# Folding the TensorE heads of the last row units, with one exponential over three heads

## The chip, the cores and the metric

The kernel runs on one core of one Trainium2 chip. The metric is the device time of one execution in microseconds, as the median of several runs; lower is better. The engines are named as in the profile: PE (TensorE's products), PEld (its weight loads), ACT (ScalarE), DVE (VectorE), POOL (GpSimd), SP (SyncE, which issues the loads).

## The reference

The input x has the shape 8 x 2048 x 2048, in float32. A row of 2048 columns is eight heads of 256 columns; each head has its own bias of 256 values. The result is, for every row and head, the logarithm of the sum of exponentials of x + bias, and each result is written twice:

```python
x_heads = x.reshape(B, S, H, Dh).transpose(0, 2, 1, 3)
x_heads = x_heads + bias[None, :, None, :]
x_tiled = np.repeat(x_heads, 2, axis=2)
mx = x_tiled.max(axis=-1, keepdims=True)
lse = mx.squeeze(-1) + np.log(np.exp(x_tiled - mx).sum(axis=-1))
```

The kernel takes no maximum: it sums exp(x + bias) directly, or exp(x) times exp(bias), and takes the logarithm at the end.

## The kernel before

**Tiles and loads.** The 16384 rows are 64 tiles of 256 rows (`T`), two rows on each of 128 partitions. Tiles lie in eight buffers (`NBUF`) and are loaded by SP, up to tile 41 in pairs of 4 MB, then singly, and from tile 57 on row by row. A row unit of 128 rows is 1 MB; the text calls the units of tile 62 "62a" and "62b", and so on. The two units of the last tile come in pieces of columns (`LAST_COLS`): 63a as columns 0-512, 1280-2048, 512-1280, and 63b in five pieces. A load waits for the last uses of the tile eight before it.

**Who adds the bias and who sums.** `STAGES` says from which tile on which mode holds. A mode's `pe` is the number of heads whose bias TensorE adds: `put_bias` (L284; L267 in the bulk) writes the bias rows into a PSUM bank as a product of three rows of ones, and `add_x` (L302; L326 in the bulk) adds x by a product with the identity matrix. ScalarE then takes the exponential out of PSUM; `sum_biased` (L357) does this for one head and gives its sum by an accumulator, which costs a second, short read-out instruction. Heads from `g0` on get their bias from GpSimd (L376). All other heads get no bias: ScalarE takes exp(x) in place (`exp_inplace`, L382), and VectorE multiplies by exp(bias) and sums in one instruction per head (`weigh`, L417). Of these, the last `fold` heads go to GpSimd instead: `fold` multiplies them by exp(bias) (L433), adds halves to halves until 32 columns are left (L441, three adds), and VectorE sums these 32 (`add_up`, L447).

- Up to tile 53 (`BULK`): three TensorE heads, four GpSimd heads, one scaled by VectorE, and one VectorE sum over seven heads (L401).
- Tiles 54 to 56 (`MIXED`): one TensorE head, four GpSimd heads.
- Tiles 57 to 61 (`PROMPT_F1`): two TensorE heads, five VectorE heads, one folded.
- 62a and 62b (`SINGLE_F1`): one TensorE head, six VectorE heads, one folded.
- 63a (`PROMPT_F2`): two TensorE heads, four VectorE heads, two folded. 63b (`TRIPLE`): three TensorE heads, five VectorE heads.

**What sets the order.** The whole order is written out by hand (`tc.manual_schedule()`): every engine runs its instructions in the order in which the loop over tiles and pieces emits them, and waits come from the data. Two lists put work off: `for_pe` holds `pe_part`, a unit's exponentials out of PSUM, which ScalarE runs behind the next unit's exponential; `for_pool` holds VectorE's sum of a fold and the next loads, which run at the start of the next unit. For each unit the loop emits TensorE's add, the next unit's bias (`put_bias`), six warming products (`keep_warm`, L317: three float32 products, two records each), `for_pool`, ScalarE's exponential, `for_pe`, and VectorE's products. PSUM has four banks in two pairs for these units; a bias may be written into a bank only after ScalarE has read what was there. `on_bank` takes away false dependences between two banks of a pair.

**The end.** Behind a batch, `finish` turns the sums by four transposes on TensorE (L461), and ScalarE takes the logarithm (L471). For the last batch `finish_last` does it with one transpose (L482), one logarithm (L488) and a store.

Of the kernel before, what the change touches and what calls it, by code (L numbers as in the profile page):

```python
# [12 lines left out]
ALU = mybir.AluOpType  # L13
# [19 lines left out]
BULK = dict(pe=3, acc=1, g0=4, late=True, fold=0)  # L33
MIXED = dict(pe=1, acc=1, g0=4, late=False, fold=0)
PROMPT_F1 = dict(pe=2, acc=2, g0=8, late=False, fold=1)
PROMPT_F2 = dict(pe=2, acc=2, g0=8, late=False, fold=2)
SINGLE_F1 = dict(pe=1, acc=1, g0=8, late=False, fold=1)
TRIPLE = dict(pe=3, acc=3, g0=8, late=False, fold=0)
FOLD = 32

# [1 line left out]
    (0, (BULK,)),  # L42
    (54, (MIXED,)),
    (57, (PROMPT_F1, PROMPT_F1)),
    (62, (SINGLE_F1, SINGLE_F1)),
    (63, (PROMPT_F2, TRIPLE)),
]

LAST_COLS = [
    [(0, 512), (1280, 2048), (512, 1280)],  # L50
    [(0, 512), (768, 1280), (1280, 1792), (512, 768), (1792, 2048)],
]

# [2 lines left out]
def kernel(  # L56
# [184 lines left out]
    n_ps = [0]  # L241


    bank_users = [[], []]

    def on_bank(i, ins):
        for j, u in bank_users[i // 2]:
            if j != i and u.ins.engine != ins.ins.engine:
                tc.declare_no_dep(ins.ins, u.ins, reason="another bank")
        bank_users[i // 2].append((i, ins))  # L250
        return ins

    def put_bias(m, k0, k1):

        if m["late"]:
            pair = pairs[n_ps[0] % 2]
            n_ps[0] += 1
            got = [one_ps, pair[:, 0:MM], pair[:, MM : 2 * MM]]  # L260

            parts = [(ones3, b3)]
            if n_ps[0] <= NEARLY:
                parts = [(ones3[0:1], bparts[:, i]) for i in range(3)]
            for h, p in enumerate(got):
                for i, (lhsT, b) in enumerate(parts):
                    nc.tensor.matmul(  # L267
                        p,
                        lhsT=lhsT,
                        rhs=each_row(b, h * Dh, Dh, K),  # L270
                        start=i == 0,
                        stop=False,
                    )
            return got + [pair]
        n = m["pe"] * Dh
        rows = min(k1 - k0, max(MM // n, 1))
        got = []
        for k in range(k0, k1, rows):
            for c in range(0, n, MM):
                w = min(n - c, MM)  # L280
                bank = n_ps[0] % len(ps)
                p = ps[bank][:, 0 : rows * w]
                n_ps[0] += 1
                mm = nc.tensor.matmul(  # L284
                    p,
                    lhsT=ones3,
                    rhs=each_row(b3, c, w, rows),
                    start=True,
                    stop=False,
                )  # L290
                on_bank(bank, mm)
                got.append((k, k + rows, c, w, bank, p))
        return got

    def add_x(m, t, k0, c0, c1, got):
# [3 lines left out]
        for ka, kb, c, w, bank, p in got:  # L299
# [10 lines left out]
            for i in range(0, (kb - ka) * w, Dh):  # L310
                k, cw = divmod(i, w)
                heads.append((ka + k, (c + cw) // Dh, bank, p[:, i : i + Dh], mm))
        return heads

    def keep_warm():
        for _ in range(NWARM):
# [112 lines left out]
    def fold(t, k, h0, h1, sums, after):  # L429


        v = xts[t % NBUF][:, k, h0 * Dh : h1 * Dh]
        done = nc.gpsimd.tensor_tensor(  # L433
            out=v, in0=v, in1=w_sb[:, h0 * Dh - W1 : h1 * Dh - W1], op=ALU.mult
        )
        on_x(t, done, [after])
        v = v.rearrange("p (h j) -> p h j", j=Dh)
        n = Dh
        while n > FOLD:
            n //= 2  # L440
            done = nc.gpsimd.tensor_tensor(  # L441
                out=v[:, :, 0:n], in0=v[:, :, 0:n], in1=v[:, :, n : 2 * n], op=ALU.add
            )
            on_x(t, done, [])

        def add_up():
            red = nc.vector.tensor_reduce(  # L447
# [55 lines left out]

    for_pool = []
    for_pe = []


    next_units = [
# [12 lines left out]
    for t in range(T):  # L521
# [4 lines left out]
        for k0, k1, c0, c1 in pieces(t):  # L526
# [5 lines left out]
            if m["late"]:  # L532
                pe_part = late_heads(m, t, bias_here, sums)
            else:
                heads = add_x(m, t, k0, c0, c1, bias_here)

                def pe_part(t=t, heads=heads, sums=sums):
                    for k, h, bank, p, mm in heads:
                        sum_biased(t, k, h, bank, p, mm, sums)

            if c0 == 0:
                if next_units and not m["late"]:
                    bias_there = put_bias(*next_units.pop(0))
                if t > T_PROMPT and m["g0"] == H:
                    keep_warm()
                if m["g0"] < H:
                    add = g_add(m, t, k0, k1)
                if t < T - 1 or k0 == 0:
                    flush(for_pool)
            if t == T_PROMPT and (k0, c0) == (0, 0):  # L550
                first_factors()
            h0 = max(c0 // Dh, m["pe"])
# [2 lines left out]
            if h0 < h1 and not m["late"]:  # L555
# [72 lines left out]
```

The softmax here doesn't subtract the row's maximum and nothing guards it: scores larger than these inputs give would overflow.

## Time and profile before

| | us |
|---|---|
| median of 4 runs (all: 325.65, 325.17, 325.19, 325.11) | 325.18 |
| the profiled execution | 325.65 |
| its span, first to last instruction | 323.5 |
| busy in the span: PE, DVE, ACT, POOL | 273.2, 283.9, 265.6, 287.7 |
| TensorE's mean granted clock | 0.903 |
| bytes read from HBM | 134.23 MB, mean 419 GB/s |

The span is what the views show; some 2 us of the time lie around it. The granted clock is the share of full speed that TensorE was given, and it was 1.00 or 0.50 in this trace. A line of the stretches gives the busy time of each engine between two times. A line of the chain gives start, length, and what the end was waiting for. A line in order of time gives start, length, engine, line of the kernel, operation, output and input, shapes, a count, and in brackets how long the engine was idle before and what ended it. A group gives the count, the busy time and the mean ns of one, the idle time before, and who ended it. TensorE's ends are modelled and its products are pipelined, so one starts before the one ahead has ended.

### The profile page before, as it was taken

To read this page: it belongs to the slowest core of one execution; us is meant where nothing else is said; L and a number is where in the kernel's file an instruction comes from. 1 tells how busy PE (TensorE), PEld (TensorE's weight loads), DVE (VectorE), ACT (ScalarE), POOL (GpSimd) and SP (SyncE) were. 2 spreads that over 40 slices of the span, in tenths; PEclk is the share of its full clock that TensorE was granted. 3 is DMA by queue.
4 is the path that set the end of the run, shared out by engine and by line. 5 is a ranking of instruction groups with operands and counts; after the bars stand their busy time and mean duration, and the time that the engine had idled before them with its cause. 6 is when DMAs were issued, how large, how long until landed. Compare 5 with 4: busy or idle time off the path is not lost.

```text
span 323.5 us, 2398 instructions
## 1 busy us (share of the span) xinstructions
PE 273.2 (84%) x691; PEld 104.0 (32%) x691; DVE 283.9 (88%) x306; ACT 265.6 (82%) x426; POOL 287.7 (89%) x120
## 2 busy tenths in 40 slices
PE   5999999889978779878679799698998897499984
PEld 2333333333323223323223233223333332135442
DVE  1037679999999998989998799998999999999995
ACT  1167679898978977879886989879898898989995
POOL 7939997999999899999999999999999999957874
PEclk9997789989997998979996979988999799559999
DMA  7999999999999999999999999999999999999994
GB/s 311 460 401 450 446 403 447 438 409 450 438 405 454 436 405 447 442 409 443 446 405 437 446 409 442 421 423 423 428 436 426 421 425 428 417 422 422 418 400 156
DMA packets 8830, 135.42 MB, mean 419 GB/s; under 512 B 1041, under 2 KB 1425, under 8 KB 2417
## 3 DMA queue, kind: packets, MB, share of 16 engines
q1 hardware_dynamic: 8720, 135.27, 98.4%
q8 instruction: 5, 0.08, 0.1%
q14 instruction: 7, 0.06, 0.0%
q10 hardware_dynamic: 98, 0.01, 0.0%
HBM read 134.23 MB, written 1.05 MB: 418 GB/s over the span
## 4 chain that ended last, share of the span: by engine, by line
DMA 34%; DVE 23%; PE 23%; ACT 18%; POOL 1%; issue 0%; SPq 0%; DVEq 0%
DMA xb<-in_x_dram 33%; DVE R L401 18%; ACT xb L382 11%; PE pair L326 8%; PE one_ps L326 4%; PE pair L267 3%; DVE xb L394 3%; ACT xb L357 2%; PE one_ps L267 2%; PE pair L302 2%; ACT xb L344 2%; DVE xb L417 2%; ACT res L471 2%; POOL xb L376 1%; ACT xb L337 1%; PE pair L219 1%
## 5 line engine op out<-in xcount | busy, mean ns | idle before, releaser
L376 POOL TENSOR_TENSOR xb<-xb,b_rep 128x2048 f32<-128x2048 f32 x57 | 257.6, 4542 | 20.6 <-DMA xb<-in_x_dram 20.6
L401 DVE TENSOR_REDUCE R<-xb 128x14 f32<-128x3584 f32 (+1 forms) x56 | 214.5, 3830 | 1.9
L382 ACT ACTIVATE xb<-xb 128x2560 f32<-128x2560 f32 (+5 forms) x77 | 157.3, 2052 | 10.0 <-POOL xb L376 10.0
L326 PE MATMUL pair<-xb,ident 128*128 128x512 f32 x216 | 116.5, 667 | 0.0
L326 PE MATMUL one_ps<-xb,ident 128*128 128x512 f32 x108 | 68.6, 721 | 9.1 <-DMA xb<-in_x_dram 8.9
L344 ACT ACTIVATE xb<-pair 128x1024 f32<-128x1024 f32 x54 | 55.9, 1036 | 24.2 <-PE pair L326 23.9
L326 PEld LDWEIGHTS pair<-xb,ident 128*128 128x128 f32 x216 | 47.3, 219 | 62.8 <-issue 62.8
L394 DVE TENSOR_TENSOR xb<-xb,w_ps 128x512 f32<-128x512 f32 x54 | 36.8, 681 | 27.1 <-ACT xb L382 26.8
L337 ACT ACTIVATE xb<-one_ps 128x256 f32<-128x256 f32 x108 | 40.3, 386 | 6.0 <-PE one_ps L326 6.0
L267 PEld LDWEIGHTS <-ones 3*128 3x128 bf16 (+1 forms) x192 | 16.7, 94 | 79.6 <-issue 70.3
L267 PE MATMUL one_ps<-b,ones 3*128 3x512 bf16 x49 | 18.5, 377 | 23.6 <-ACT xb L337 23.6
L267 PE MATMUL pair<-b,ones 3*128 3x512 bf16 x98 | 28.9, 374 | 0.0
L326 PEld LDWEIGHTS one_ps<-xb,ident 128*128 128x128 f32 x108 | 17.4, 202 | 31.5 <-issue 16.2
L302 PE MATMUL pair<-xb,ident 128*128 128x512 f32 (+1 forms) x36 | 21.6, 687 | 6.7 <-DMA xb<-in_x_dram 6.7
L337 ACT ACTIVATION_READ_ACCUMULATOR xb<-one_ps 128x1 f32 x108 | 22.9, 212 | 0.0
L417 DVE CUSTOM_DVE_ANT_0 xb<-xb,w_ps 128x256 f32<-128x256 f32 x61 | 22.4, 418 | 0.0
L441 POOL TENSOR_TENSOR xb<-xb 128x128 f32<-128x128 f32 (+3 forms) x39 | 13.8, 355 | 3.1
L433 POOL TENSOR_TENSOR xb<-xb,w_sb 128x256 f32<-128x256 f32 (+1 forms) x13 | 10.0, 772 | 5.7 <-ACT xb L382 5.1
L317 PE MATMUL tp<-ident 128*128 128x128 f32 x84 | 13.9, 304 | 0.0
L317 PEld LDWEIGHTS tp<-ident 128*128 128x128 f32 x84 | 11.3, 203 | 3.7 <-issue 3.3
L471 ACT ACTIVATE res<-tp 32x1024 f32<-32x1024 f32 x7 | 7.1, 1013 | 5.9 <-PE tp L461 5.9
L357 ACT ACTIVATE xb<-pair 128x256 f32<-128x256 f32 x33 | 11.9, 362 | 0.0
(42 smaller groups left out, 86.9 us busy)
## 6 DMA issues: line engine op xcount, KB each, us to landing
xb<-in_x_dram SPq DMA_DIRECT2D x20, 4096.0 KB, 21.8
xb<-in_x_dram SPq DMA_DIRECT2D x17, 2048.0 KB, 21.6
xb<-in_x_dram SPq DMA_DIRECT2D x12, 1024.0 KB, 22.0
xb<-in_x_dram SPq DMA_DIRECT2D x4, 256.0 KB, 13.2
out_dram<-res SPq DMA_DIRECT2D x1, 896.0 KB, 6.7
xb<-in_x_dram SPq DMA_DIRECT2D x2, 384.0 KB, 15.9
xb<-in_x_dram SPq DMA_DIRECT2D x2, 128.0 KB, 6.3
out_dram<-res_last SPq DMA_DIRECT2D x1, 128.0 KB, 1.7
```

What stands on the lines that cost most here:

```text
L267: nc.tensor.matmul(p, lhsT=lhsT, rhs=each_row(b, h * Dh, Dh, K), start=i == 0, stop=False,)
L302: mm = nc.tensor.matmul(p, lhsT=ident, rhs=xts[t % NBUF][:, ka:kb, c : c + w], start=False, stop=True,)
L317: nc.tensor.matmul(tp[:, 0], lhsT=ident, rhs=ident, start=True, stop=True)
L326: mm = nc.tensor.matmul(p, lhsT=ident, rhs=xts[t % NBUF][:, :, h * Dh : (h + 1) * Dh], start=False, stop=True,)
L337: act = nc.scalar.activation(out=xts[t % NBUF][:, k, 0:Dh], in_=got[0][:, k * Dh : (k + 1) * Dh], func=ACT.Exp, accum_out=sums[:, k, 0:1],)
L344: act = nc.scalar.activation(out=xts[t % NBUF][:, :, Dh : m["pe"] * Dh].rearrange("p k (h j) -> p h k j", j=Dh), in_=got[-1].rearrange("p ...
L357: act = nc.scalar.activation(out=xts[t % NBUF][:, k, h * Dh : (h + 1) * Dh], in_=p, func=ACT.Exp, accum_out=sums[:, k, h : h + 1],)
L376: add = nc.gpsimd.tensor_tensor(out=v, in0=v, in1=each_row(b_rep, c - G0, D - c, k1 - k0), op=ALU.add)
L382: return on_x(t, nc.scalar.activation(out=v, in_=v, func=ACT.Exp), [after])
L394: mul = nc.vector.tensor_tensor(out=f, in0=f, in1=each_row(w_ps, m["pe"] * Dh - W0, n, k1 - k0), op=ALU.mult,)
L401: red = nc.vector.tensor_reduce(out=sums[:, k0:k1, h0:H], in_=v.rearrange("p k (h j) -> p k h j", j=Dh), op=ALU.add, axis=mybir.AxisListTy ...
L417: ttr = nc.vector.tensor_tensor_reduce(out=v, in0=v, in1=w, scale=1.0, scalar=0.0, op0=ALU.mult, op1=ALU.add, accum_out=dst,)
```

## The change

In units 62a, 62b and 63a a new mode, `FOLDED`, takes the place of `SINGLE_F1` and `PROMPT_F2`. TensorE adds the bias to three heads (768 columns, a whole pair of banks). The new `exp_biased` takes their exponential in one ScalarE instruction over 768 columns, without accumulators, and GpSimd folds all three heads; since their bias is already in, the multiplication (L433 before) is left out. VectorE multiplies and sums the other five heads; no head without a TensorE bias is folded in these units.

The order changes too. In 62a and 62b the exponential out of PSUM runs directly behind the unit's own exponential, ahead of the next unit's. VectorE's sum of a fold is held back by one more unit (`held`). Units with three TensorE heads have no warming products any more, as `m["pe"] * Dh <= MM` is false for them. In all units from tile 54 on, the next unit's bias is emitted behind the warming products and behind `for_pe` instead of ahead of them. In 63a the first piece has 768 columns instead of 512 and the third 512 instead of 768. 63b is unchanged.

```diff
-PROMPT_F2 = dict(pe=2, acc=2, g0=8, late=False, fold=2)
-SINGLE_F1 = dict(pe=1, acc=1, g0=8, late=False, fold=1)
+FOLDED = dict(pe=3, acc=0, g0=8, late=False, fold=0)
...
-    (62, (SINGLE_F1, SINGLE_F1)),
-    (63, (PROMPT_F2, TRIPLE)),
+    (62, (FOLDED, FOLDED)),
+    (63, (FOLDED, TRIPLE)),
...
-    [(0, 512), (1280, 2048), (512, 1280)],
+    [(0, 768), (1280, 2048), (768, 1280)],
...
         n = m["pe"] * Dh
+        if n > MM:
+            n_ps[0] += n_ps[0] % 2
...
+    def exp_biased(t, k, n, heads):
+
+        _, _, bank, _, mm = heads[-1]
+        act = nc.scalar.activation(
+            out=xts[t % NBUF][:, k, 0 : n * Dh],
+            in_=pairs[bank // 2][:, 0 : n * Dh],
+            func=ACT.Exp,
+        )
+        on_bank(bank, on_x(t, act, [mm]), both=True)
+        return act
...
-        done = nc.gpsimd.tensor_tensor(
-            out=v, in0=v, in1=w_sb[:, h0 * Dh - W1 : h1 * Dh - W1], op=ALU.mult
-        )
-        on_x(t, done, [after])
+        done = after
+        if h0 * Dh >= W1:
+            mul = nc.gpsimd.tensor_tensor(
+                out=v, in0=v, in1=w_sb[:, h0 * Dh - W1 : h1 * Dh - W1], op=ALU.mult
+            )
+            done = on_x(t, mul, [done])
...
-                def pe_part(t=t, heads=heads, sums=sums):
+                def pe_part(t=t, m=m, k=k0, heads=heads, sums=sums):
+                    if m["acc"] == 0:
+                        done = exp_biased(t, k, m["pe"], heads)
+                        for_pool.append(fold(t, k, 0, m["pe"], sums, done))
+                        return
                     for k, h, bank, p, mm in heads:
                         sum_biased(t, k, h, bank, p, mm, sums)
...
-                if next_units and not m["late"]:
-                    bias_there = put_bias(*next_units.pop(0))
-                if t > T_PROMPT and m["g0"] == H:
+                if t > T_PROMPT and m["g0"] == H and m["pe"] * Dh <= MM:
                     keep_warm()
...
-                if t < T - 1 or k0 == 0:
+                if m["acc"] == 0 and for_pool and last_acc == 0:
+
+                    held = list(for_pool)
+                    for_pool.clear()
+                elif t < T - 1 or k0 == 0:
                     flush(for_pool)
+                last_acc = m["acc"]
...
-            if c0 == 0:
+            if m["acc"] == 0 and t < T - 1:
+                for_pe.append(pe_part)
+            if c0 == 0 or t == T - 1 and k0 == 0:
                 flush(for_pe)
+            if c0 == 0 and next_units and not m["late"]:
+                bias_there = put_bias(*next_units.pop(0))
...
+                if h0 < h1:
+                    flush(held)
...
-            elif heads:
+            elif heads and not (m["acc"] == 0 and t < T - 1):
                 for_pe.append(pe_part)
```

More of the change, by code (lines that the diff above doesn't have):

```diff
@@ L244, with on_bank @@
     bank_users = [[], []]
-    def on_bank(i, ins):
-        for j, u in bank_users[i // 2]:
-            if j != i and u.ins.engine != ins.ins.engine:
+    def on_bank(i, ins, both=False):
+        pair = i // 2
+        i = None if both else i
+        for j, u in bank_users[pair]:
+            if None not in (i, j) and j != i and u.ins.engine != ins.ins.engine:
                 tc.declare_no_dep(ins.ins, u.ins, reason="another bank")
-        bank_users[i // 2].append((i, ins))
+        bank_users[pair].append((i, ins))
         return ins
@@ L440, in fold @@
             n //= 2
-            done = nc.gpsimd.tensor_tensor(
+            add = nc.gpsimd.tensor_tensor(
                 out=v[:, :, 0:n], in0=v[:, :, 0:n], in1=v[:, :, n : 2 * n], op=ALU.add
             )
-            on_x(t, done, [])
+            done = on_x(t, add, [done])
         def add_up():
@@ L505 @@
     for_pe = []
+    held = []
+    last_acc = None
     next_units = [
```

## The prediction

> **What bounds the kernel now.** I read the load on each engine first, then the stretches of the end, then the chain that ended last, then the single rows of that chain. The loads use the DMA engines for nearly the whole span, but the last bytes are there before 318 us, and the change touches only the four row units behind that (62a, 62b, 63a, 63b). So the question is what the last 12 us wait for.
>
> ```profile
> q1 hardware_dynamic: 8720, 135.27, 98.4%
> ```
>
> Columns of the next view: stretch, its length, busy us (instructions) of PE, PEld, DVE, ACT, POOL, then granted clock, DMA share, GB/s.
>
> ```profile
> 300.00:305.00 5.00, 5.00 (x26) 2.96 (x26) 5.00 (x32) 5.00 (x13) 4.22 (x10) 1.00 1.02 424
> 310.00:315.00 5.00, 4.26 (x20) 2.31 (x20) 4.73 (x28) 5.00 (x14) 3.91 (x9) 1.00 1.03 393
> 315.00:320.00 5.00, 3.34 (x19) 2.13 (x18) 4.96 (x30) 4.78 (x17) 4.03 (x8) 1.00 0.73 256
> ```
>
> ScalarE (ACT) has no idle time and VectorE (DVE) almost none: both bound the end, so taking work from one alone gains little. The chain (start, length, what) shows the hand-over:
>
> ```profile
> 292.87 1.01 ACT res L471
> ...
> 310.58 1.59 ACT xb L382
> 312.17 0.71 ACT xb L357 x4
> 312.88 1.60 ACT xb L382
> 314.48 0.02 issue
> 314.50 0.42 DVE xb L417
> ...
> 319.83 0.14 DVE R_last L447
> ```
>
> From 293 to 314 ACT is the chain, from there VectorE's products, to 319.97. Single rows in order of time:
>
> ```profile
> 292.87 1.01 ACT L471 ACTIVATE res<-tp 32x1024 f32<-32x1024 f32 x1 [0.51 <-PE tp L461]
> 310.49 1.68 ACT L382 ACTIVATE xb<-xb 128x1792 f32<-128x1792 f32 x1
> 311.97 0.19 DVE L447 TENSOR_REDUCE R_last<-xb 128x1 f32<-128x32 f32 x1 [0.19 <-POOL xb L441]
> 312.34 0.70 PE L302 MATMUL pair<-xb,ident 128*128 128x256 f32 x2 [0.74 <-DMA xb<-in_x_dram]
> 314.06 1.02 PE L302 MATMUL pair<-xb,ident 128*128 128x512 f32 x2
> 315.02 0.49 PE L284 MATMUL pair<-b,ones 3*128 3x512 bf16 x2
> 317.85 1.65 POOL L441 TENSOR_TENSOR xb<-xb 128x256 f32<-128x256 f32 x3
> ```
>
> The first row is the one place where the saturated part of ACT stood still: 0.51 us for TensorE's transposes, which ran late behind half-clock work. The groups give what the new instructions cost:
>
> ```profile
> L344 ACT ACTIVATE xb<-pair 128x1024 f32<-128x1024 f32 x54 | 55.9, 1036 | 24.2 <-PE pair L326 23.9
> L441 POOL TENSOR_TENSOR xb<-xb 128x256 f32<-128x256 f32 x1 | 0.7, 725 | 0.1
> L441 POOL TENSOR_TENSOR xb<-xb 128x128 f32<-128x128 f32 x12 | 5.5, 457 | 0.9
> ```
>
> **The change, part by part.**
>
> *ACT.* Before, 62a to the end takes 16 exponentials, nine of them sums from PSUM (L357, one per 0.36 us). After, it takes 15, five of them sums. The columns are the same; four read-outs go, and 9.2 us of work becomes 8.9. Prices: 1280 columns lie between rows of 1536 (1466 ns) and 768 (827 ns), 0.83 ns a column: 1.25 us. The new 768 columns from PSUM: the 1024-column row is 1036 ns, less 256 x 0.83 = 0.82 us. The bounds are 0.78 (from the 357 ns sum row plus 512 columns) and 0.90; I take the row without a sum. Back to back, each starts 0.09 before the end of the one ahead.
>
> *TensorE.* A unit now needs two bias products and a 512- and a 256-column add. From the rows above: biases 0.23 + 0.20, add records 0.53 + 0.43 + 0.22 and 0.38 to the end of the last: 1.98 us, against 0.28 + 0.70. Each unit takes a whole pair of banks, so 62a's second bias waits for 61a's sum (310.58), 62b's first for 61b's sum (312.45). Behind a waiting bias stands the whole queue: its add, then the later units. 24 warming products (L317, 0.77 us a unit) go.
>
> *GpSimd.* Three multiplications go (0.73, 0.73, 1.28). Adds are over 384, 192 and 96 elements: (725 - 457) / 128 = 2.1 ns an element gives 0.99, 0.59 and 0.39, with two gaps of 0.08: 2.13 us a unit. Bounds: 1.65, the two-head row, with which VectorE's wait for it goes (325.2), and 2.5, half as much again, with which 62b's fold and all behind it come 0.74 later (326.3). I take the line through the two rows.
>
> *VectorE.* 20 products instead of 21, at 0.342 (rows 312.20 to 314.25 hold six), three sums over 96 elements instead of 32, 32, 64: about 0.17 against 0.10 of queue time, 0.25 for the last. Its work falls by 0.1 us.
>
> *The walk*, in the times of the profile, 62a's exponential starting at 310.49 as now:
> - ACT: 62a 310.49-311.74; 61b's two sums to 312.36; TensorE has 62a at 312.40, so the folded exponential runs 312.44-313.26. 62b 313.17-314.42. TensorE, held by 61b's sum, ends 62b at 314.50: folded 314.54-315.36 (wait 0.21). 63a's 768 columns 315.27-316.09; TensorE ends 63a at 316.41: folded 316.45-317.27 (wait 0.45). Then 512, 512, 512, 256 end at 317.79, 318.31, 318.83, 319.14; three sums end at 320.2.
> - GpSimd: 313.34-315.46, 315.47-317.60, 317.60-319.73.
> - VectorE: 61b's sum at 311.97, 62a's five products 312.07-313.78; waits for 62b's exponential, 314.45-316.16; sum of 62a's fold to 316.33; three products of 63a to 317.36; now **62b's fold (317.60) holds the queue**; sum to 317.82; two and five products to 320.21; last sum to 320.46.
>
> Against 319.96 that is +0.50: the folded exponentials ahead of 62b's own, and GpSimd, which starts 1.1 us later than now (313.34 against 312.24), put two waits of 0.67 and 0.27 into VectorE where it had none.
>
> *The stall at 292.87.* The warming products now come before the next bias. I count TensorE's full-height stream (products over 128 rows, not the three-row biases): 0.43 us for a 512-column record, 0.11 for a 128-column one, their spacing in the rows at full clock, and double at half. The clock's stretches are 3.41 us. In 284.86-288.28 this was an add (1.71 us) and the warming products up to the edge (0.65): 0.69 of the stretch, and the clock stayed at 0.50. The next held 0.76 and it rose. After, the add and all six (1.28) lie in the first: 0.87, so the clock should rise at 288.28, and the transposes be done well before ACT asks at 292.25. Then ACT's whole end moves 0.62 earlier (292.87 - 292.25); VectorE's queue is full until 311.70, its 62a then starts at 311.80, 62b's at 313.83, and the walk ends at 319.85.
>
> *Edits costed at nothing:* 63a's pieces of 384, 384, 256 KB instead of 256, 384, 384: three loads before and after on SP's queue, same bytes, 2.5 us a MB (TensorE's waits of 309.83 and 312.34), so they land by 313.3, 314.2 and 314.9, and the walk asks at 314.4 or later. The bias behind the warming in units 57 to 61: TensorE takes 2.04 a unit against ACT's 2.09 and fills banks units ahead; if that cover went, one bias and its switch, 0.31 a unit. VectorE's later sums: covered by products, except where the walk shows the fold late.
>
> *The sum.* The profiled execution took 325.65: its span of 323.5 and 2.15 around it. Its own stall removed and the walk's loss added: 325.65 - 0.11 = 325.54. The other three runs (325.11, 325.17, 325.19) are 0.47 faster. Without the stall the kernel before would itself end sooner: 62b's exponential would start when its load lands (312.30) and end at 314.0, VectorE at 319.48, that is 0.48 sooner. So I take those runs to have had no stall, and add 319.85 - 319.48 = 0.37 to the median of 325.18: **325.55 us**.
>
> *A rule against a row.* In 271.21-274.62 TensorE was busy 2.49 of 3.41 us, and the next stretch was granted 0.50: the clock fell without an idle stretch. The Trainium skill, "TensorE: Matmul & The Clock Gate", Part 1, says it falls back after at least one idle window of about 3.4 us. By the rule the end of the changed kernel, idle for 1.9 us at most, is safe and the sum stands at 325.55; by the row the third rival below stays possible.
>
> **The rivals.** 0.2% here is 0.65 us, about what a measurement can tell from no change. That the change does not do what it says I leave out: the changed kernel's instruction lists show the folded exponentials, the missing multiplications and the later sums where the code puts them.
> - *Stall gone only by the change* (B): the 0.47 between the runs is the profiler's cost and all runs before had the stall. For it: four runs can't tell. Then 325.18 - 0.11 = 325.07.
> - *Stall stays after the change* (C), because the clock's stretches lie otherwise: 320.46 against 319.48, 326.16.
> - *The clock falls in the tail* (D), the one that ends clearly slower. Between 61b's warming (ends near 308.95) and 62a's add (310.84, or 310.2 without the stall) TensorE has nothing tall to do. Stretches of the bulk whose full-height stream was up to 0.37 of 3.41 us were followed by 0.50, from 0.40 on by 1.00; a stretch from 308.95 to 312.36 would hold 1.28 us, 0.375. It decides from there. Against it: with the stretches where the profile has them (308.76) it is 0.43 or more. Price: 62b's and most of 63a's add at half rate, 63a's folded exponential 1.6 later, and the seven products behind it: 327.2.
> - *Better than walked* (E): TensorE's or GpSimd's waits don't arise. VectorE is still held by 62b's exponential, and 15 products and the sums behind it end at 320.10 - 0.62 = 319.5: no change. Faster by over 0.2% needs the stall to have been longer in the ordinary runs than in the profile: below 324.5.
>
> **How the numbers follow.** As forecast (325.55, own range 325.2 to 326.3 by GpSimd's bounds, which are the widest): 50 in 100, 6 of them above 325.83. B 18, C 14, D 12, E 6. Faster 0.06; slower 6 + 14 + 12 = 0.32; within 0.62. The range leaves out D and E: 324.9 to 326.4.
>
> **What would show it.** Right: folded exponentials near 0.82 us, the second and third waiting for TensorE; three GpSimd adds near 0.99, 0.59, 0.39; VectorE waiting once for ACT and once for GpSimd before its last seven products; no wait of L471's counterpart, and clock 1.00 from about 288. Wrong: VectorE without gaps to the end, ACT never waiting for TensorE, a half-clock stretch behind 309, or a last product that ends before 319.5.

## The result, and the profile after

The changed kernel takes **325.73 us** (median of 34 runs, 325.52 to 327.45), the kernel before, measured beside it, 325.37 us (55 runs, 325.07 to 326.71). The ratio is 1.0012, with a 95% interval of 1.0006 to 1.0018: slower by 0.2 to 0.6 us, and inside the 0.2% that the prediction took for no change. The forecast was 325.55, and the step from before to after +0.37; the medians differ by 0.36. The close agreement is partly luck: two errors in the working nearly cancelled, the waits that it named were not what cost the time, and the kernel before, which it took to run mostly without its stall, has a median of 325.37 and not 325.18.

The profiled execution took 325.71 us (span 323.7). First the stretches of the end, with the columns as before (stretch, length, busy us and instructions of PE, PEld, DVE, ACT, POOL, granted clock, DMA share, GB/s):

```profile
310.00:315.00 5.00, 4.74 (x15) 2.07 (x15) 4.81 (x24) 4.88 (x10) 3.23 (x8) 1.00 1.03 391
315.00:320.00 5.00, 2.92 (x10) 0.95 (x8) 5.00 (x29) 4.32 (x12) 4.13 (x7) 1.00 0.78 252
```

In the last 5 us ScalarE now has idle time (4.32 us busy against 4.78), VectorE none. The chain that ended last, start, length, what:

```profile
292.50 0.89 ACT res L488
...
308.00 1.38 ACT xb L397
...
311.47 0.19 DVE R_last L464
...
313.01 1.08 DVE xb L432
...
315.47 0.79 DVE xb L432
...
320.02 0.18 DVE R_last L464
```

From 311.47 to 320.19, where VectorE's last row ends, the chain is VectorE's own queue, without a wait. But two products in it take 1.08 and 0.79 us of the chain, where the others take 0.33. The same place as single rows, put together from the rows of ScalarE, GpSimd and VectorE in order of time:

```profile
292.39 1.00 ACT L488 ACTIVATE res<-tp 32x1024 f32<-32x1024 f32 x1
311.93 0.81 ACT L322 ACTIVATE xb<-pair 128x768 f32<-128x768 f32 x1
312.81 6.63 POOL L458 TENSOR_TENSOR xb<-xb 128x384 f32<-128x384 f32 x9 [1.38 <-ACT xb L322]
312.93 1.17 DVE L432 CUSTOM_DVE_ANT_0 xb<-xb,w_sb 128x256 f32<-128x256 f32 x1
314.02 0.81 ACT L322 ACTIVATE xb<-pair 128x768 f32<-128x768 f32 x1
315.40 0.86 DVE L432 CUSTOM_DVE_ANT_0 xb<-xb,w_sb 128x256 f32<-128x256 f32 x1
315.93 0.81 ACT L322 ACTIVATE xb<-pair 128x768 f32<-128x768 f32 x1 [0.37 <-PE pair L306]
316.19 0.24 DVE L464 TENSOR_REDUCE R_last<-xb 128x3 f32<-128x96 f32 x1
317.04 0.42 DVE L432 CUSTOM_DVE_ANT_0 xb<-xb,w_sb 128x256 f32<-128x256 f32 x1
317.39 0.24 DVE L464 TENSOR_REDUCE R_last<-xb 128x3 f32<-128x96 f32 x1
319.94 0.25 DVE L464 TENSOR_REDUCE R_last<-xb 128x3 f32<-128x96 f32 x1
```

What to see: the logarithm (L488) starts with no idle time in brackets, so the stall of 0.51 us is gone. The folded exponentials take 0.81 us, as forecast. The long products are those whose second input is `w_sb`: the factor of head 7, the only factor of these heads that lies in SBUF and not in PSUM. Both long ones run while GpSimd adds, and the sums of the folds (L464) have no wait at all. The groups of 312 to 320, kept apart by shape (count, busy us and mean ns, idle before), give GpSimd's adds and the two kinds of product:

```profile
L458 POOL TENSOR_TENSOR xb<-xb 128x384 f32<-128x384 f32 x3 | 3.2, 1064 | 1.4 <-ACT xb L322 1.4
L458 POOL TENSOR_TENSOR xb<-xb 128x192 f32<-128x192 f32 x3 | 1.9, 634 | 0.2
L458 POOL TENSOR_TENSOR xb<-xb 128x96 f32<-128x96 f32 x3 | 1.2, 385 | 0.2
...
L432 DVE CUSTOM_DVE_ANT_0 xb<-xb,w_ps 128x256 f32<-128x256 f32 x15 | 5.4, 410 | 0.0
L432 DVE CUSTOM_DVE_ANT_0 xb<-xb,w_sb 128x256 f32<-128x256 f32 x4 | 2.9, 716 | 0.0
```

The same groups in the kernel before, also 312 to 320:

```profile
L417 DVE CUSTOM_DVE_ANT_0 xb<-xb,w_ps 128x256 f32<-128x256 f32 x15 | 5.4, 417 | 0.0
L417 DVE CUSTOM_DVE_ANT_0 xb<-xb,one_ps 128x256 f32<-128x256 f32 x5 | 1.9, 418 | 0.1
...
L417 DVE CUSTOM_DVE_ANT_0 xb<-xb,w_sb 128x256 f32<-128x256 f32 x1 | 0.4, 422 | 0.0
```

`one_ps` and `w_ps` lie in PSUM, and the six products of 62a from 312.20 on are among these 20. There is one product by `w_sb`, at 319.40, as the very last: head 7 of the other units was folded there, and it was GpSimd that multiplied by `w_sb`. The change folds heads 0 to 2 instead, and so hands head 7 of 62a, 62b and 63a to VectorE.

### The profile page after: what moved, and what is told of

Its sections match the earlier page's. It is cut to its first block, busy times and chain, and to the rows that moved or that the text cites. A ratio compares the mean times of both kernels' runs of the same rounds, so it can differ in the third digit from the quotient of the medians.

```text
span 323.7 us, 2358 instructions
## 1 busy us (share of the span) xinstructions
PE 268.6 (83%) x676; PEld 102.1 (32%) x676; DVE 284.6 (88%) x304; ACT 265.3 (82%) x421; POOL 287.7 (89%) x117
## 4 chain that ended last, share of the span: by engine, by line
DMA 35%; DVE 20%; POOL 17%; PE 14%; ACT 13%; issue 0%; SPq 0%; DVEq 0%
DMA xb<-in_x_dram 34%; POOL xb L391 17%; DVE R L416 14%; ACT xb L397 9%; PE pair L341 5%; PE one_ps L341 3%; PE pair L269 3%; DVE xb L432 2%; DVE xb L409 2%; ACT xb L372 2%; PE one_ps L269 1%; PE pair L218 1%; DMA brow<-in_bias_dram 1%; ACT xb L352 1%; ACT xb L359 1%; ACT res L488 1%
## 5 line engine op out<-in xcount | busy, mean ns | idle before, releaser
L341 PE MATMUL pair<-xb,ident 128*128 128x512 f32 x216 | 114.5, 657 | 0.0
L341 PE MATMUL one_ps<-xb,ident 128*128 128x512 f32 x108 | 67.7, 712 | 10.7 <-DMA xb<-in_x_dram 10.7
L341 PEld LDWEIGHTS pair<-xb,ident 128*128 128x128 f32 x216 | 46.0, 213 | 61.7 <-issue 61.7
L306 PE MATMUL pair<-xb,ident 128*128 128x512 f32 (+1 forms) x42 | 23.7, 665 | 4.6 <-DMA xb<-in_x_dram 4.6
L458 POOL TENSOR_TENSOR xb<-xb 128x128 f32<-128x128 f32 (+5 forms) x39 | 16.4, 424 | 4.2 <-ACT xb L322 1.4
L306 PEld LDWEIGHTS pair<-xb,ident 128*128 128x128 f32 x42 | 7.1, 206 | 14.5 <-DMA xb<-in_x_dram 11.1
L450 POOL TENSOR_TENSOR xb<-xb,w_sb 128x256 f32<-128x256 f32 x10 | 7.3, 729 | 4.5 <-ACT xb L397 3.8
L332 PEld LDWEIGHTS tp<-ident 128*128 128x128 f32 x60 | 8.6, 198 | 7.4 <-issue 4.9
L372 ACT ACTIVATE xb<-pair 128x256 f32<-128x256 f32 x29 | 10.5, 367 | 0.0
L488 ACT ACTIVATE res<-tp 32x1024 f32<-32x1024 f32 x7 | 7.1, 1011 | 4.1 <-PE tp L478 4.1
```

What stands on the lines that cost most here:

```text
L306: mm = nc.tensor.matmul(p, lhsT=ident, rhs=xts[t % NBUF][:, ka:kb, c : c + w], start=False, stop=True,)
L341: mm = nc.tensor.matmul(p, lhsT=ident, rhs=xts[t % NBUF][:, :, h * Dh : (h + 1) * Dh], start=False, stop=True,)
L372: act = nc.scalar.activation(out=xts[t % NBUF][:, k, h * Dh : (h + 1) * Dh], in_=p, func=ACT.Exp, accum_out=sums[:, k, h : h + 1],)
L458: add = nc.gpsimd.tensor_tensor(out=v[:, :, 0:n], in0=v[:, :, 0:n], in1=v[:, :, n : 2 * n], op=ALU.add)
```

## The experiments

Theory P: the products by `w_sb` are held up by GpSimd's adds (they "stand"), and this is what the walk of the forecast lacked. Rivals: GpSimd's fold holds VectorE's sums (the forecast's own step), or the order of ScalarE costs the time. A second question is the stall before the logarithm, and whether the order of the bias took it away.

| kernel | us, median | before, beside it | ratio, 95% interval | us from the end of 62b's exponential to the end of VectorE's last row |
|---|---|---|---|---|
| changed | 325.73 | 325.37 | 1.0006 to 1.0018 | 6.30 |
| no folding adds | 325.47 | 325.40 | 0.9997 to 1.0022 | 6.04 |
| factor in PSUM from tile 59 | 325.78 | 325.40 | 1.0003 to 1.0025 | 6.70 |
| four moves | 325.30 | 325.36 | 0.9991 to 1.0014 | 5.73 |
| the factor's two moves alone | 325.61 | 325.41 | 1.0003 to 1.0024 | 6.04 |
| the order's two moves alone | 325.77 | 325.41 | 1.0006 to 1.0023 | 6.29 |
| folded exponentials late | 326.94 | 325.36 | 1.0031 to 1.0057 | 7.78 |
| changed, old order of the bias | 325.70 | 325.40 | 1.0003 to 1.0020 | 6.28 |
| before, new order of the bias | 325.15 | 325.40 | 0.9990 to 1.0020 | 5.50 |
| the same again | 325.29 | 325.41 | 0.9997 to 1.0030 | 5.50 |
| before, later logarithm | 325.65 | 325.36 | 1.0000 to 1.0017 | |
| before, both | 325.43 | 325.36 | 0.9995 to 1.0020 | |
| two folded units | 325.60 | 325.41 | 1.0003 to 1.0020 | 6.43 |

The last column is read from each profiled execution and leaves out what happened earlier in it. With no wait, the changed kernel's queue there is 15 products at 0.342, two sums at 0.17 and the last at 0.25: 5.72 us.

**GpSimd's nine adds left out.**

```diff
-        while n > FOLD:
+        while n > FOLD and h0:
```

> The changed kernel without GpSimd's nine additions in 62a, 62b and 63a; VectorE's three sums take the first 32 columns of each folded head as they are, so these heads' results leave out 224 of 256 columns. The eighth head's factor stays in SBUF. Theory P (a VectorE product with both inputs in SBUF stands until GpSimd's addition has ended): the eighth head's products take 0.42 us, and VectorE has only the waits for ScalarE left, ending near 319.9 instead of 320.19: 0.2 to 0.3 us faster than the changed kernel (1.0002 to 1.0006). Theory Q (another cause): the products stay long. If GpSimd alone were the bound of the end, the gain would be larger than 0.5 us, since its last addition ended at 319.45.

The four products by `w_sb` take 421 ns on average instead of 716, and VectorE now stands only for ScalarE:

```profile
312.87 0.42 DVE L432 CUSTOM_DVE_ANT_0 xb<-xb,w_sb 128x256 f32<-128x256 f32 x1
313.86 0.42 DVE L432 CUSTOM_DVE_ANT_0 xb<-xb,w_ps 128x256 f32<-128x256 f32 x1 [0.56 <-ACT xb L397]
315.23 0.42 DVE L432 CUSTOM_DVE_ANT_0 xb<-xb,w_sb 128x256 f32<-128x256 f32 x1
317.22 0.42 DVE L432 CUSTOM_DVE_ANT_0 xb<-xb,w_ps 128x256 f32<-128x256 f32 x1 [0.20 <-ACT xb L397]
```

So it is GpSimd's adds that make them long. The 0.74 us of 62a's product bought little, since VectorE then waits 0.56 for 62b's exponential; the 0.44 of 62b's counted, less 0.20 that VectorE then waits for 63a's. Seven of the 11 runs lie below the lowest of the changed kernel's 34 (325.52).

**The factor of head 7 in PSUM from tile 59 on.**

```diff
-            w = w_sb[:, c - W1 : c - W1 + Dh]
+            w = one_ps[:, 0:Dh]
...
+        if t == 59:
+            nc.vector.tensor_copy(one_ps[:, 0:Dh], w_sb[:, W2 - W1 :])
```

> The changed kernel, with the factor of the eighth head (columns 1792 to 2048) copied once, by VectorE in tile 59, into a half of a PSUM bank whose factor is no longer needed, and read there by VectorE's products; before it lay in SBUF. Theory P (a VectorE product with both inputs in SBUF stands until GpSimd's running addition has ended): the eighth head's products take 0.42 us instead of 1.17 and 0.86, VectorE is through 62b's products by 315.7 instead of 316.2, then waits for GpSimd's fold of 62b near 317.2 as the prediction had it, and ends near 320.05 instead of 320.19: the median falls by 0.05 to 0.2 us against the changed kernel (1.0006 to 1.0010 against the kernel before). Theory Q (these products are long for another cause, such as the unit's exponential or a bank of PSUM): they stay long and the time stays 1.0012.

The products took 414 to 417 ns while GpSimd added, and GpSimd's own first adds 998 to 1010 ns, the second ones 592 instead of 634. The time did not fall, though Theory P had expected it to: the copy took 0.42 us of a VectorE that is nearly full from tile 57 on, and in this execution its whole queue was late (its last long sum, over the GpSimd heads ahead of tile 57, ran at 292.34, in the changed kernel at 290.51). The cause of the length was shown, its worth was not; in the next two runs the copy lies in a gap, and the third leaves the factor where it was.

**Four moves in the tail.** 62a's head 7 first, before GpSimd adds; the copy behind 62a's products, where VectorE waits anyway; 63a's folded exponential behind its last own exponential; VectorE's sum of 62b's fold behind all of 63a's products.

```diff
+    first_w7 = []
...
+        elif not first_w7:
+            first_w7.append(t)
+            w = w_sb[:, c - W1 : c - W1 + Dh]
         else:
-            w = w_sb[:, c - W1 : c - W1 + Dh]
+            w = one_ps[:, 0:Dh]
...
-            if c0 == 0 or t == T - 1 and k0 == 0:
+            if c0 == 0 or t == T - 1 and k0 == 0 and c0 == 3 * Dh:
                 flush(for_pe)
...
-                    for h in range(h0, hf):
+                    hs = list(range(h0, hf))
+                    if (t, k) == (T - 2, 0):
+                        hs = hs[-1:] + hs[:-1]
+                    for h in hs:
...
-                if h0 < h1:
+                if h0 < h1 and (t < T - 1 or c0 == 3 * Dh):
                     flush(held)
+                if (t, k0) == (T - 2, 0):
+                    nc.vector.tensor_copy(one_ps[:, 0:Dh], w_sb[:, W2 - W1 :])
```

> The changed kernel with four places in its tail moved, each after a wait or a long product that its trace shows: 62a's head 7 is multiplied first, before GpSimd adds; the factor of head 7 is copied to PSUM in VectorE's gap behind 62a's products, so that 62b's and 63a's head 7 read one operand from PSUM; 63a's folded exponential stands behind its last own exponential; VectorE's sum of 62b's fold stands behind all of 63a's products. Theory P (VectorE's products with both inputs in SBUF stand while GpSimd adds, 0.74 and 0.44 us too long): the three products take 0.42 us each, VectorE ends about 319.6 instead of 320.19, and the time is 325.2 to 325.3 us, 0.9993 to 1.0000 of the kernel before. Rival (what is saved on VectorE goes into its waits for the exponentials and for GpSimd): VectorE ends at 320.0 to 320.2 again, 325.6 to 325.75 us, 1.0006 to 1.0014.

```profile
312.18 0.81 ACT L322 ACTIVATE xb<-pair 128x768 f32<-128x768 f32 x1 [0.24 <-PE pair L306]
314.18 0.42 DVE L437 CUSTOM_DVE_ANT_0 xb<-xb,w_ps 128x256 f32<-128x256 f32 x1 [0.49 <-ACT xb L397]
319.62 0.25 DVE L469 TENSOR_REDUCE R_last<-xb 128x3 f32<-128x96 f32 x1
```

From 62b's exponential to the end VectorE needs 5.73 us, which is the sum without any wait. It ends at 319.87 and not at 319.6 because TensorE gave 62a's bank 0.24 late in this execution. The chain shows from when:

```profile
293.43 0.94 PE tp L332 x6
294.36 0.32 PE pair L288
294.68 1.73 PE pair L306 x2
...
310.65 1.50 PE pair L306 x4
```

TensorE had waited 1.35 us for ScalarE's logarithm (the warming products write the tile that it reads), its granted clock was 0.50 from 294.93 to 298.35, an add took 1.73 us of the chain instead of 1.06, and up to 312 TensorE did not catch up. Such a half-clock stretch behind the logarithm stands in three of the 14 traces here (this one, and the runs below with the folded exponentials late and with two folded units), all with the new order of the bias. The loss is gone (325.30 beside 325.36, and seven of the 11 runs below the changed kernel's lowest), but no gain is shown either.

**The factor's two moves alone.** Of the diff above only `weigh` with `first_w7`, the list `hs` and the copy; the order as changed:

```diff
+                    hs = list(range(h0, hf))
+                    if (t, k) == (T - 2, 0):
+                        hs = hs[-1:] + hs[:-1]
...
+                if (t, k0) == (T - 2, 0):
+                    nc.vector.tensor_copy(one_ps[:, 0:Dh], w_sb[:, W2 - W1 :])
```

> The changed kernel with only the first two of the four moves of the run before it (62a's head 7 first; the factor of head 7 copied to PSUM in VectorE's gap), its order otherwise as changed. Theory P (the products that stand for GpSimd cost the most of the loss, and with them gone the wait for GpSimd's fold of 62b comes up, as the prediction had it): 62b's products start at 313.9 and end at 315.7, three of 63a at 316.8, VectorE then waits 0.2 to 0.4 for GpSimd's fold (317.0 to 317.2), and ends at 319.9 instead of 320.19: about 325.45 us, 1.0001 to 1.0007 of before. Rival (the factor's place alone is worth the whole gain of the four moves): 325.3 us, and VectorE does not wait for GpSimd.

The products by either place of the factor, and then the rows in which VectorE waits:

```profile
L437 DVE CUSTOM_DVE_ANT_0 xb<-xb,one_ps 128x256 f32<-128x256 f32 x3 | 1.3, 418 | 0.0
...
L437 DVE CUSTOM_DVE_ANT_0 xb<-xb,w_sb 128x256 f32<-128x256 f32 x1 | 0.4, 415 | 0.0
```

```profile
314.01 0.42 DVE L437 CUSTOM_DVE_ANT_0 xb<-xb,w_ps 128x256 f32<-128x256 f32 x1 [0.22 <-ACT xb L397]
317.17 0.25 DVE L469 TENSOR_REDUCE R_last<-xb 128x3 f32<-128x96 f32 x1 [0.18 <-POOL xb L463]
319.76 0.25 DVE L469 TENSOR_REDUCE R_last<-xb 128x3 f32<-128x96 f32 x1
```

This is the tail that the forecast had walked: with the long products gone, VectorE has 0.64 us for ScalarE, 0.42 of it filled by the copy (0.67 was forecast), and waits 0.18 for GpSimd's fold of 62b (0.27 was forecast). So the wait of Theory P came (0.2 to 0.4 was expected), but not its time: 325.61 instead of 325.45. Beside the changed kernel's 325.73 a gain is not clear of the noise; only one of the 11 runs lies below 325.52. From the start of 62a's exponential (310.07) to the end (320.02) are 9.95 us; the walk had 309.87 and 319.85, 9.98.

**The order's two moves alone.** The other half, with the factor in SBUF:

```diff
-            if c0 == 0 or t == T - 1 and k0 == 0:
+            if c0 == 0 or t == T - 1 and k0 == 0 and c0 == 3 * Dh:
                 flush(for_pe)
...
-                if h0 < h1:
+                if h0 < h1 and (t < T - 1 or c0 == 3 * Dh):
                     flush(held)
```

> The changed kernel with only the last two of the four moves (63a's folded exponential behind its last own exponential; VectorE's sum of 62b's fold behind all of 63a's products), head 7's factor in SBUF as changed. Theory P: the products of head 7 stand for GpSimd as in the changed kernel (about 1.16 and 0.86 us), VectorE ends at 320.1 to 320.2, 325.65 to 325.75 us, 1.0009 to 1.0013 of before. Rival (the order of ScalarE and of the sums costs the loss, not the factor's place): VectorE ends at 319.7 to 319.9, 325.3 to 325.4 us.

```profile
L432 DVE CUSTOM_DVE_ANT_0 xb<-xb,w_sb 128x256 f32<-128x256 f32 x4 | 2.9, 714 | 0.0
```

ScalarE's last sum ends 0.6 us earlier than in the changed kernel (318.99 against 319.60, 0.12 of it by an earlier start), and VectorE's tail is as long as there (6.29). The order alone shows no gain; it pays once the products are short, when it takes the wait for GpSimd away: 6.04 to 5.73, one trace each.

**The folded exponentials late:** those of 62a and 62b behind the next unit's own exponential, as the kernel before orders them.

```diff
-            if m["acc"] == 0 and t < T - 1:
-                for_pe.append(pe_part)
...
-            elif heads and not (m["acc"] == 0 and t < T - 1):
+            elif heads:
```

> The changed kernel with one thing put back: the folded exponentials of 62a and 62b stand behind the next unit's own exponential on ScalarE, as the kernel before has them, and GpSimd folds as in the changed kernel. Theory W (ScalarE's order is paid for by GpSimd's room): 62b's exponential starts with its landing, about 312.3, and ends about 313.55 instead of 313.895, so VectorE waits less for it; but GpSimd's first add starts about 314.35 instead of 312.81, its nine adds (three times 1.00 + 0.66 + 0.39, and one of 1.19) end about 320.95 instead of 319.45, and VectorE's last sum of the folds ends about 321.3 instead of 320.19: about 326.8 us, 1.0040 to 1.0048 of the kernel before. Rival (ScalarE's order alone costs the loss): GpSimd's later start is hidden, VectorE ends 0.3 to 0.4 earlier than in the changed kernel: about 325.3 us, 0.9995 to 1.0002.

```profile
312.52 1.27 ACT xb L397
313.79 0.71 ACT xb L322
...
314.56 1.01 POOL xb L458
...
321.32 0.27 DVE R_last L464
```

62b's exponential starts with its landing, and GpSimd 1.75 us later than in the changed kernel (314.56 against 312.81). From there GpSimd is the chain to the end, and VectorE's last sum waits 0.77 us for it. So the early place of the folded exponentials is paid for (62b's exponential starts at 312.63 in the changed kernel and at 312.52 here, where its load landed at 312.49), but it is the cheaper of the two.

**The order of the bias.** First the changed kernel with the bias ahead of the warming products again, as far as the banks allow it; then the kernel before with only the new order.

```diff
+                early = bool(next_units) and not m["late"] and t < 61
+                if early:
+                    bias_there = put_bias(*next_units.pop(0))
...
-            if c0 == 0 and next_units and not m["late"]:
+            if c0 == 0 and next_units and not m["late"] and not early:
                 bias_there = put_bias(*next_units.pop(0))
```

> The changed kernel, with the old order of the next unit's bias up to tile 60 (ahead of the warming products and of the work put off); the folded units keep the new one, since their banks need it. Theory 1 (the new order takes the stall away): the stall of about 0.5 us before the seventh batch's logarithm is back in the trace, the clock rises a stretch of 3.41 us later, and the median is 0.1 to 0.5 us above the changed kernel's, so about 326.0 against 325.73 (1.0015 to 1.0028 against the kernel before). Theory 2 (the order does nothing in ordinary runs): 1.0012 as the changed kernel.

```diff
-                if next_units and not m["late"]:
-                    bias_there = put_bias(*next_units.pop(0))
...
+            if c0 == 0 and next_units and not m["late"]:
+                bias_there = put_bias(*next_units.pop(0))
```

> The kernel before, with only the new order of the next unit's bias: behind the warming products and behind the work put off, in all units from tile 54 on. Modes, folds and pieces stay as before. Theory 1 (the stall behind the half-clock transposes was part of the ordinary runs, more in some than in others): the logarithm of the seventh batch no longer waits for TensorE, the clock is at 1.00 from about 288 us on, and the median falls by 0.1 to 0.5 us against the kernel before (0.9985 to 0.9997), to its fastest runs near 325.1; the runs lie closer together. Theory 2 (the ordinary runs had no stall, the profiled one was slow by the profiler): no change, 1.0000 within 0.0003. Theory 3 (the bias behind the warming costs TensorE 0.31 us a unit): ScalarE waits for TensorE in units 57 to 61 and the time rises by 0.3 us or more.

> The kernel before with the new order of the bias alone, once more. If that order takes the stall before the logarithm away in most runs: again most runs at 325.04 to 325.2 us, median 0.1 to 0.25 below that of before. If the first answer was chance: a median within 0.05 of before.

In the kernel before with the new order, the logarithm and the last sum:

```profile
292.39 1.00 ACT L471 ACTIVATE res<-tp 32x1024 f32<-32x1024 f32 x1
319.28 0.22 DVE L447 TENSOR_REDUCE R_last<-xb 128x2 f32<-128x64 f32 x1
```

No stall, and VectorE ends at 319.50, where the forecast put the kernel before without its stall (319.48); the repeat ends at 319.49. The clock did what the prediction had worked out. The next two lines are the same stretch, first of the kernel before (TensorE's busy time, then clock, DMA share and GB/s), then with the new order (all engines):

```profile
288.28:291.69 3.41, 3.41 (x9) 0.50 1.02 423
288.30:291.70 3.40, 3.40 (x17) 1.91 (x16) 3.40 (x14) 3.40 (x4) 1.15 (x2) 1.00 1.01 422
```

In these two traces the stretches of the clock lie within 0.04 us of each other, and the full clock came at 288.24 instead of 291.69 (288.28 was forecast). The half clock in this part lasted five stretches of 3.41 us in the kernel before and in its run with the later logarithm below, and three or four in all 11 traces with the new order. The changed kernel with the old order is the exception: four stretches, which lay 1 us later, no stall in its trace, and the same 325.70. Of the runs of the kernel before, 21 of 97 in these comparisons lie at 325.20 or below; with the new order 13 of 23 do, and the others at 325.39 to 327.72. So the order seems to make the undisturbed case more frequent. That it makes the kernel faster is not established: both intervals reach over 1. Nor do the runs lie closer together, which the first theory had also expected: three of the 23 take 327.58 us or more.

**The logarithm three tiles later,** in the kernel before, alone and with the new order of the bias:

```diff
-        fb, at = divmod(t - 2, NBLK)
+        fb, at = divmod(t - (5 if t > T_PROMPT else 2), NBLK)
```

> The kernel before with the finish of batch 7 (transposes, logarithm, store) three tiles later, and nothing else: the transposes then come when the exponentials they follow have long been fed, whatever TensorE's clock does at 288. Theory S (the stall before the logarithm is in most ordinary runs of before, and is what its median stands above its fastest runs by): median about 325.1 us with the runs close together, 0.9990 to 0.9996 of before. Rival (the spread of the runs has another cause): 325.35 to 325.45 us, 0.9998 to 1.0003, spread as in before.

> The kernel before with the later finish of batch 7 and with the changed kernel's order of the bias (the warming products and the adds of the pairs ahead of it). Theory S: with the stall gone by the later finish the order of the bias is worth nothing more: the same 325.1 us as with the later finish alone. Rival (the order of the bias has a worth or a price of its own, by the clock it gives TensorE): it differs from the later finish alone by 0.1 us or more.

Theory S fell in its first form: alone it was no faster but slower by 0 to 0.17%. The chain of the first one says why the stall could not go away like that:

```profile
302.46 0.98 PE pair L302 x2
...
304.62 0.45 PE tp L461 x4
...
305.10 1.01 ACT res L471
```

TensorE is still the chain at 304, twelve us after its half clock: it wins only 0.05 us a unit on ScalarE, so the transposes come late at 304.6 as well, and ScalarE stands 0.1 us. With the new order as well the chain in that part is ScalarE's, and the median 325.43; the two differ by 0.22, which would fit the rival that gives the order a worth of its own, but their intervals lie almost wholly over each other, so it is not shown. Why the median of the first lies above that of the kernel before was not settled.

**Two folded units.** A version put together from what the runs showed:

```diff
+DOUBLE = dict(pe=2, acc=2, g0=8, late=False, fold=0)
...
-    (62, (FOLDED, FOLDED)),
+    (62, (DOUBLE, FOLDED)),
...
+        elif t < T - 1:
+            w = w_sb[:, c - W1 : c - W1 + Dh]
         else:
-            w = w_sb[:, c - W1 : c - W1 + Dh]
+            w = one_ps[:, 0:Dh]
...
+            if (t, k0) == (T - 2, 0):
+                nc.scalar.activation(
+                    out=one_ps[:, 0:Dh], in_=b_rep[:, W2 - G0 :], func=ACT.Exp
+                )
...
+                    if (t, k) == (T - 2, 1):
+                        hs = hs[-1:] + hs[:-1]
...
```

> A version drawn from the runs: only 62b and 63a are folded; 62a has two heads from TensorE, summed by ScalarE behind 62b's own exponential, and six on VectorE; head 7's factor is written to PSUM by ScalarE while it waits for 62b's load; 62b's head 7 first, and the tail's order of the four moves. By the rows: 62b's exponential ends at 313.6, VectorE's products run from 311.57 on without a wait to 319.2, GpSimd's second fold ends at 319.2, ScalarE's last sum and VectorE's last sum at 319.5: 0.7 before the changed kernel and level with the kernel before without its stall, 324.9 to 325.1 us, 0.9985 to 0.9997 of before. Rival (ScalarE or GpSimd becomes the end): their last ends lie at 319.8 or later, 325.3 us or more.

```profile
312.42 0.42 DVE L435 CUSTOM_DVE_ANT_0 xb<-xb,one_ps 128x256 f32<-128x256 f32 x1 [0.77 <-ACT one_ps L595]
319.76 0.25 DVE L467 TENSOR_REDUCE R_last<-xb 128x3 f32<-128x96 f32 x1
```

Neither theory had what happened. VectorE's first product of 62a reads head 2's factor, the other half of the PSUM tile `one_ps` that ScalarE had just been given to write, and waited 0.77 us for that write; from 312.42 on VectorE had no gap. Without that wait GpSimd's last add (319.36) and the sum behind it would end at 319.6, an estimate from these rows, 0.1 behind the 319.50 of the kernel before with the new order; that was not run.

## Why the prediction was right, and where it was not

*The sum.* The step of +0.37 stood against 0.36 in the medians. But the forecast's step was meant against a kernel before without its stall. Against the kernel before with the new order of the bias, whose traces have none, the medians differ by 0.58 and 0.44 (325.15 and 325.29), and VectorE's end by 0.70 (320.19 against 319.50). Two terms make the difference to 0.37. The whole end lay 0.12 later than walked (62a's exponential at 309.99, not 309.87), because ScalarE's part without idle time began 0.13 later in this execution than in the profile before (287.11 against 286.98); the kernel before does not pay this, since its 62b waits for the landing at 312.3 anyway. And from the start of 62a's exponential to the end it took 10.20 us, 0.22 longer than walked.

*The step that failed* is in the part on VectorE: "20 products instead of 21, at 0.342 (rows 312.20 to 314.25 hold six)". All six rows of that price have their factor in PSUM. Four of the 20 new products do not, three more than before, and two of these three took 1.17 and 0.86 us. With that, the second of the two waits ("62b's fold (317.60) holds the queue", 0.27) did not occur in the changed kernel: VectorE reached that sum at 317.39, when the fold had been done for 0.2 us. And the first, 0.67 for 62b's exponential, did not show, since the long product of 62a filled it. "VectorE without gaps to the end" had been named as a sign against the forecast, and it came. Two errors nearly cancelled: the walk had waits of 0.94 us that did not come, and lacked 1.18 us of longer products that did. The run with the factor's two moves shows both waits as soon as the products are short.

Nor does the loss lie where the forecast put it, in 62b's exponential behind the folded one. Against the kernel before with the new order, 62b's exponential started 0.34 later but has 512 columns fewer, and ended 0.10 earlier (313.90 against 314.00). The whole loss is in VectorE's queue behind it, 6.30 us against 5.50. Of these 0.80, 0.22 would be there without any wait (5.72, with three sums over 96 columns in place of two over 32 and 64); most of the rest are the long products, about 0.1 of 62a's, which ended after 62b's exponential, and 0.44 of 62b's.

*Right:* the folded exponentials (0.81 for 0.82); GpSimd's adds (1.00, 0.59 and 0.39 where no product is in their way); the second and third folded exponential waiting for TensorE (0.12 and 0.37 for 0.21 and 0.45); the late start of 62b's exponential (312.63 for 312.55); the stall gone, with the full clock from 287.4 (288.28 forecast); the pieces of 63a, whose loads nobody waited for.

*Wrong in a reason:* "TensorE takes 2.04 a unit against ACT's 2.09 and fills banks units ahead". It does not get ahead, as the run with the later logarithm shows; in the changed kernel this cost nothing, with the four moves 0.24 us in the profiled execution. And "I take those runs to have had no stall" fits the three runs it spoke of (their 325.11 to 325.19 is where the version without the stall lies), but not the median: over more runs the kernel before spreads to 326.7, and its median is 325.37. Two small sums do not come out either, and neither moves the forecast: without the wait for GpSimd the end is 0.27 earlier, at 325.28 and not 325.2; and in "Better than walked" the 15 products and the sums end at 320.17 by the prediction's own prices, not at 320.10.

*The rivals.* Stall gone only by the change (325.07): no run of 34 came below 325.52, and the kernel before has runs down to 325.07 itself. Stall stays (326.16): no. The clock falling in the tail (327.2): it was granted 1.00 from 287.4 to 321.5. A fall did occur elsewhere, near 295, in the three traces named above, behind a wait of TensorE of only 1.35 to 1.91 us: as in the prediction's row at 271, no idle stretch of 3.41 us was needed. Better than walked: VectorE's tail was longer, not shorter.

## What to carry to other kernels

When work moves between engines, list where each operand of the moved instructions lies, not only how many there are: a price from rows with a PSUM operand says nothing of the same instruction with two SBUF inputs beside a busy GpSimd. Where a full queue shows no waits but its rows change in length, compare the rows by operand; a stand inside an instruction is not in the list of waits. And one remedy can show no gain until another has been made: the order of the tail paid only after the factor had moved.

## What the runs showed of the hardware

A VectorE product with two SBUF inputs that started while a GpSimd add ran did not end until 0.28 us behind that add. The first line is such an add in the changed kernel, beside the product of 1.17 us; the second is a product in the run with the folded exponentials late, beside the add at 314.56:

```profile
312.81 1.00 POOL L458 TENSOR_TENSOR xb<-xb 128x384 f32<-128x384 f32 x1 [1.38 <-ACT xb L322]
315.19 0.66 DVE L432 CUSTOM_DVE_ANT_0 xb<-xb,w_sb 128x256 f32<-128x256 f32 x1
```

Add and product end at 313.815 and 314.099, 315.976 and 316.260 in the changed kernel, at 313.694 and 313.977, 315.852 and 316.136 with the order's two moves, at 315.567 and 315.848 with the folded exponentials late: 0.28 us each time, wherever in the add the product began. So the length goes by what is left of the add: 63a's product began 0.14 us before its add ended (317.176), ended 0.28 behind it, and took its usual 0.42. The other way round, the add that starts 0.1 us behind this product (317.13) takes 1.19 us instead of 1.00. With the factor in PSUM neither is lengthened (418 and 1004 ns).

The Trainium skill, "SBUF — State Buffer", section "SBUF: two separate sides", says that VectorE and GpSimd share a pair of SBUF ports as an exclusive lock, held for the whole instruction by whichever comes first, and counts VectorE instructions with two SBUF inputs among those that take it, against a GpSimd instruction that reads SBUF. The runs agree for the product behind the add. For the add behind the product they show 0.19 us, less than the 0.33 that was left of the product. The rule spoke against this change, and the prediction did not use it.
